# A mixed RWKV-7 and GatedDeltaNet layer on one core: the first branch's scan rebuilt on prepared transition matrices

## The chip, the core and the metric

The kernel runs on one core of one Trainium2 chip. The metric is the device time of one execution in microseconds. A matmul runs on TensorE (PE in the profile; its weight loads are PEld), elementwise work on VectorE (DVE), ScalarE (ACT) and GpSimd (POOL); SyncE (SP) issues most of the DMAs. Each engine works through its own instructions in order and waits on semaphores for what others have made.

## The reference

One layer over 256 latent tokens and 256 context tokens, width D = 2048. Latent and context tokens are normalised and modulated, projected by one weight `w_in`, and go through two token mixers, each in both directions. The context is scanned first and its final state starts the latent scan. Cut to what matters:

```python
mod = silu(c) @ w_ada + b_ada            # shifts, scales, gates (and the same for c_ctx)
h, hc = modulate(rmsnorm(x), ...), modulate(rmsnorm(ctx), ...)
rw, cv, z, ab, gt = split(h @ w_in)      # the same for hc

# first branch, RWKV-7: 16 heads of 64, per token and direction
def step(s, (r, w, k, v, kk, b)):        # s is 64 x 64
    sa = s @ kk
    s  = s * w - outer(sa, b) + outer(v, k)
    return s, s @ r

# second branch, gated DeltaNet (GDN): 8 heads of 128, in chunks of 64, with a
# triangular solve per chunk and a scan over chunks of the same kind
y = (sigmoid(g_a) * (o_a @ p_a) + sigmoid(g_b) * (o_b @ p_b)) @ w_out
x = x + gt1 * y
x = x + gt2 * swiglu(modulate(rmsnorm(x)))
return rmsnorm(x)
```

The decays `w` and the rates in `b` and `k` come from low-rank products (ranks 96, 96 and 64). All arithmetic is float32.

## The kernel before

A large projection is split: each float32 operand is a high and a low part of a faster type, and each k-tile of 128 takes three matmuls, `hxh` by `whi`, `hxl` by `whi`, `hxh` by `wlo`. One product has 16 k-tiles, so 48 matmuls, 512 columns wide (all tokens: the letters k, v, K, V) or 256 (latent tokens: r, Q and the gates g). `cast` loads its weights (`wraw`), rounds them to `whi` on ACT and subtracts on DVE to get `wlo`. Small matmuls are plain float32, and the profile shows two records for one of them.

The stages are, in order: modulation and the low-rank inputs (a first stage limited by the loads of `w_ada`, whose parts are woven with small products by the table `TILES`, lines 521 to 535); the weave, in which both branches run beside the projections; then the products with `p_a`, `p_b` and `w_out`, the FFN and the last norm.

In the weave, two RWKV heads make a pair, which occupies the 128 partitions, and there are 8 pairs. Tokens lie in 8 chunks of 64, the first four latent and the last four context. For pair `p` the work goes through generators:

- `prepare(p)` makes the keys, rates and decays: `exc` and `inc` are running products of decays up to and including a token, `et` their ends. It builds the operands: `LAl` (latent keys by `exc` and receptance by `inc`, in one tile per direction), `LAc` (context keys by `exc`), `ic` and `kt`.
- `grams(p, d)` multiplies them within a chunk, masks, and keeps the triangle `LT`, the masked products in place of `LAl`/`LAc`, and `Pm`; it turns `ic` and `kt` into `KB`.
- `inverse(p)` inverts the unit triangles (`invert`, by 16-token blocks, then 32, then 64) and multiplies the inverse into `KB` and `Pm`.
- `values(p)` (not changed) and `scan(p)`: the scan walks over 8 chunks in both directions at once, four context chunks and then four latent ones. `VX` holds state and values of a chunk. Per step, `VX` by `LAc` or `LAl` gives a first sum, which ACT copies into `VX`; a second group multiplies by `KB`, adds an identity product that carries the state, and DVE multiplies by `et` into the next `VX`. In the latent steps the readout (`LAl` by `VX`, then `Pm` by `VX`) is added and goes to `Y`.

GDN heads go through `tokens` (operands `keg`, `kta`), `head_grams`, `head_inverse` and `head_scan` (`NW` holds the products for the steps) in the same way, 8 heads in turn, after the last pairs.

What sets the order of instructions on PE, DVE and ACT is a planner, the class `Weave` (lines 185 to 281). Each generator yields one operation or a list for one engine; a tuple such as `("scan", p - 3)` waits until that name has been called ready, and a bank name waits for a free PSUM bank. The planner keeps a clock per engine with a cost for each operation, takes the operation that can start first, and breaks ties by rank (`RANK`, line 30: lower first). What it picks is written down as the program. Of the large products, `products` chooses the next one when the one before starts. The order of SP's queue follows from the same run, since the loads are issued as generators reach them.

## Time and profile before

| | |
|---|---|
| median of 3 runs | 2216.26 us (2205.15 to 2219.96) |
| the profiled execution | 2212.82 us, span 2211.0 us |
| PE busy | 2138.1 us (97%) |
| DVE busy | 1560.2 us (71%) |
| ACT busy | 1081.2 us (49%) |
| POOL busy | 93.6 us (4%) |
| DMA | mean 197 GB/s, 435.13 MB |

The first stage lasts to about 118 us, the weave from there to 1244 us, where the products with `p_a` begin; the FFN lies between 1452 and 1950 us, and the last product and norm behind it. The inverses of the 8 pairs end at 277, 353, 421, 488, 555, 623, 687 and 752 us and their scans at 312, 390, 461, 524, 595, 659, 723 and 789 us. The second branch's scans begin between 865 and 1261 us.

In a row of the profile `s<-VX,KB 128*64 128x64 f32 x8` means: written to `s` (a PSUM bank) from `VX` and `KB`, with 128 rows and 64 columns of the array in use, 128 partitions by 64 columns moving, eight records in a row. A start and a duration in us stand ahead; in square brackets stands the idle time before it and what ended it. L147 is the line of the planner's helper that issues every planned operation, so most rows of the weave have it. Durations of matmuls overlap, so lengths are taken from starts.

### The profile page before, as it was taken

The page shows a single profiled execution, that of the slowest core. Times are in us where ns is not written, and L with a number is a line of the kernel's source. Part 1 is how long each engine was busy: PE and PEld are TensorE (multiplying, and loading weights), DVE is VectorE, ACT ScalarE, POOL GpSimd, SP SyncE. Part 2 cuts the span into 40 slices and gives each one's busy share as a digit, 9 for nine tenths or more (in the row PEclk, how much of TensorE's full clock was granted, in tenths as well). Part 3 has the DMA queues.
Part 4 walks back from the last instruction along what each step waited for, and adds up shares of the span by engine and source line. Part 5 has one row for each costly group of instructions (what it writes and reads, how often), then busy time and mean ns, then how long its engine had stood idle before and what let it go on. Part 6 is the DMA issues. An engine that isn't in the chain of part 4 may idle for free. (4 is left out here: it accounts for less than half of the span.)

```text
span 2211.0 us, 54434 instructions
## 1 busy us (share of the span) xinstructions
PE 2138.1 (97%) x22780; PEld 1910.8 (86%) x22780; DVE 1560.2 (71%) x3245; ACT 1081.2 (49%) x1915; POOL 93.6 (4%) x171
## 2 busy tenths in 40 slices
PE   6998999999999999999899899999999999999998
PEld 4776678787788788887789799999999999999997
DVE  3456788888798577998998689956665655444444
ACT  3248745545456555454554465534444444444443
POOL 0000000000000010111110010100000000000000
PEclk9999899999999999999999999999999999999999
DMA  9966544444444355565567888927777776566665
GB/s 383 413 188 201 152 117 108 120 109 109 121 113 112 111 182 167 177 195 167 170 202 251 291 297 303 344 78 236 237 235 233 230 234 198 186 184 187 188 185 160
DMA packets 234486, 435.13 MB, mean 197 GB/s; under 512 B 115329, under 2 KB 129665, under 8 KB 229889
## 3 DMA queue, kind: packets, MB, share of 16 engines
q1 hardware_dynamic: 206304, 355.11, 51.1%
q0 software_dynamic: 14112, 51.39, 7.1%
q10 hardware_dynamic: 13824, 25.17, 3.4%
q8 instruction: 178, 2.92, 0.6%
q14 instruction: 68, 0.55, 0.1%
HBM read 405.76 MB, written 25.84 MB: 195 GB/s over the span
## 5 line engine op out<-in xcount | busy, mean ns | idle before, releaser
L371 DVE TENSOR_TENSOR wlo<-wraw,whi 128x1024 fp32r<-128x1024 f32 x328 | 392.7, 1198 | 319.5 <-ACT whi L370 317.4
L370 ACT CAST whi<-wraw 128x1024 fp32r<-128x1024 f32 x328 | 337.9, 1031 | 461.3 <-PE mm L381 410.6
L147 PE MATMUL mm<-hxh,wlo 128*128 128x256 f32 (+1 forms) x1376 | 460.6, 335 | 5.7 <-DVE wlo L147 5.5
L147 PE MATMUL mm<-hxh,whi 128*128 128x256 f32 (+1 forms) x1376 | 461.9, 336 | 0.9 <-ACT arena L147 0.5
L147 PE MATMUL mm<-hxl,whi 128*128 128x256 f32 (+1 forms) x1376 | 460.8, 335 | 0.0
L380 PE MATMUL mm<-hfh,whi 128*128 128x256 f32 x1344 | 376.8, 280 | 0.0
L381 PE MATMUL mm<-hfl,whi 128*128 128x256 f32 x1344 | 375.8, 280 | 0.0
L382 PE MATMUL mm<-hfh,wlo 128*128 128x256 f32 x1344 | 374.6, 279 | 0.1
L147 PEld LDWEIGHTS mm<-hxh,wlo 128*128 128x128 f32 x1376 | 260.1, 189 | 33.6 <-DVE wlo L147 8.4
L147 PEld LDWEIGHTS mm<-hxh,whi 128*128 128x128 f32 x1376 | 260.1, 189 | 27.1 <-issue 4.4
L147 PEld LDWEIGHTS mm<-hxl,whi 128*128 128x128 f32 x1376 | 260.2, 189 | 26.1 <-issue 6.2
L147 DVE TENSOR_TENSOR wlo<-wraw,whi 128x512 fp32r<-128x512 f32 x344 | 236.9, 691 | 49.5 <-ACT whi L147 48.0
L382 PEld LDWEIGHTS mm<-hfh,wlo 128*128 128x128 f32 x1344 | 252.6, 188 | 0.6 <-DVE wlo L371 0.5
L381 PEld LDWEIGHTS mm<-hfl,whi 128*128 128x128 f32 x1344 | 252.7, 188 | 0.0
L380 PEld LDWEIGHTS mm<-hfh,whi 128*128 128x128 f32 x1344 | 252.5, 188 | 0.0
L147 ACT CAST whi<-wraw 128x512 fp32r<-128x512 f32 x344 | 205.2, 616 | 96.2 <-PE mm L147 63.4
L147 DVE TENSOR_TENSOR arena<-arena 128x28 f32<-128x28 f32 (+13 forms) x538 | 132.1, 247 | 18.7 <-DMA arena<-scr 7.1
L380 PE MATMUL mm<-za,whi 128*128 128x256 f32 x512 | 144.0, 281 | 0.0
L381 PE MATMUL mm<-za,whi 128*128 128x256 f32 x512 | 143.3, 280 | 0.0
L382 PE MATMUL mm<-za,wlo 128*128 128x256 f32 x512 | 142.4, 278 | 0.0
L147 ACT ACTIVATE arena<-arena 128x512 f32<-128x512 f32 (+3 forms) x132 | 76.8, 592 | 40.1 <-DVE arena L147 37.3
L381 PEld LDWEIGHTS mm<-za,whi 128*128 128x128 f32 x512 | 96.3, 188 | 0.0
(329 smaller groups left out, 3911.3 us busy)
## 6 DMA issues: line engine op xcount, KB each, us to landing
wraw<-w SPq DMA_DIRECT2D x172, 512.0 KB, 4.3
wraw<-wgu SPq DMA_DIRECT2D x168, 512.0 KB, 4.7
aw<-ada_rest POOLq DMA_DIRECT2D x96, 512.0 KB, 5.5
aw<-ada_first SPq DMA_DIRECT2D x32, 1024.0 KB, 12.6
wraw<-wdn SPq DMA_DIRECT2D x64, 448.0 KB, 3.6
wraw<-wout SPq DMA_DIRECT2D x32, 512.0 KB, 6.3
aw<-ada_gt ACTq DMA_DIRECT2D x64, 256.0 KB, 4.9
wraw<-wdn SPq DMA_DIRECT2D x32, 512.0 KB, 3.6
```

Of the source, the lines that this page charges most:

```text
L147: return Op(self, cost, lambda: getattr(self.engine, name)(out, *a, **k), kind)
L370: S.copy(hi[:, c, :M], raw[:, c, :M])
L371: V.tensor_sub(lo[:, c, :M], raw[:, c, :M], hi[:, c, :M].bitcast(F32))
L380: E.matmul(ps, hi, Xh[:, k, :n], start=first and i == 0, stop=False)
L381: E.matmul(ps, hi, Xl[:, k, :n], start=False, stop=False)
L382: E.matmul(ps, lo, Xh[:, k, :n], start=False, stop=last and i == len(wt) - 1)
```

## The change

`prepare(p)` no longer makes `LAl` and `LAc`. It makes `kh` (all keys by `exc`, one 128x512 multiplication per direction) and `laR` (receptance by `inc`). For direction 0 it now waits for `scan(p-2)` instead of `scan(p-3)`, ahead of `et`, `kh` and `laR`.

`grams(p, d)` has a first group over all 8 chunks (`ic` by `kh`, `kh` by `kt`) and a second one with the receptance over the four latent chunks. The masked key product goes to a new tile `X`, into which `kh` is also turned (four more transposes and four ACT copies per direction). A new tile `KBx` is filled with identities by two POOL copies per pair; the turned `kt` goes into its other halves. It waits for `("mats", p - 2)` in direction 0 and for `("begun", p)` in direction 1.

`inverse(p)` ends with three more groups of 32 matmuls of 64x64x64, `X` by `KB` for each direction and `X` by `Pm`, each followed by two DVE additions of 512 columns into `KBx` and `laR`. After that, `KBx` holds for each chunk and direction a full 128x128 transition matrix. The copy of `Pm` moves from DVE to ACT, and `KB` is copied at once. In `invert` the second product of the 16-unit case is 64 matmuls of 32x32 by 16 columns instead of 32 of 64x64 by 16.

`scan(p)` has 7 steps, each of two matmuls 128x128x128 (one per direction) and two DVE multiplications by `et`, and then one readout of 16 matmuls into one bank and one `Y` copy.

In the second branch `NW` has three blocks instead of four per direction, `keg` and `kta` have 384 instead of 512 columns in half of their multiplications, and several buffers share the place of `X`. `products` chooses the next product at k-tile 4 of the current one instead of at its start, and r of a pair needs `("kgemm", p)` instead of `("prepared", p-1, 0)`. `TILES` and the loads of the first stage go in pairs.

```diff
--- invert, scan's waits, products, TILES
-        TILES = ((0, 0, 0, 0), (1, 1, 1, 1), ...
+        TILES = ((0, 0), (2, 2), (2, 2), (2, 2), (1, 3), (2, 2), (1, 3), (1, 2), (2, 2))
...
-        if nu == 16:
-            yield [e.matmul(pv[64 * h:64 * h + 64, 1, u], Tx[64 * h:64 * h + 64, u, :], Qm[64 * h:64 * h + 64, u, :],
-                            start=True, stop=True) for u in range(nu) for h in range(2)]
-        else:
-            yield [e.matmul(pv[r, 1, u], Tx[r, u, b:b + 32], Qm[r, u, :], start=True, stop=True) for h, u, b, r in fours]
+        yield [e.matmul(pv[r, 1, u], Tx[r, u, b:b + 32], Qm[r, u, :], start=True, stop=True) for h, u, b, r in fours]
...
                 if p > 1:
                     yield "inverse", p - 2
-                if p > 2:
-                    yield "scan", p - 3
+                if p > 1:
+                    yield "scan", p - 2
+                o["laR"] = la = rs.tile([P, 2, 4, 2, 64], F32, tag="laR", name="laR", bufs=2)
...
+            o["kh", d] = kh = rs.tile([P, 512], F32, tag="Kh", name="kh", bufs=2)
+            yield v.tensor_mul(c3(kh), c3(kk), exc)
             for j, h in enumerate(half):
-                yield v.tensor_mul(la[h, :, j, 0:64], c3(kk)[h, 0:4, :], exc[h, 0:4, :])
-                yield v.tensor_mul(la[h, :, j, 64:P], c3(r)[h], inc[h, 0:4, :])
-                yield v.tensor_mul(lc[h, :, j, :], c3(kk)[h, 4:8, :], exc[h, 4:8, :])
+                yield v.tensor_mul(la[h, d, :, j, :], c3(r)[h], inc[h, 0:4, :])
...
+        yield from turn(kh, 0, 4, lambda j, i, w: s.copy(X[half[1 - j], d, i::2, j, :], w))
         if d == 0:
             if p:
                 yield ("scan", p - 2) if p > 1 else ("lowrank", NPAIR - 1)
-            o["KB"] = rs.tile([P, 2, 8, 2, 64], F32, tag="KB", name="KB", bufs=2)
+            o["KB"] = rs.tile([P, 2, 8, 64], F32, tag="KB", name="KB", bufs=2)
+            o["KBx"] = KBx = rs.tile([P, 2, 8, 2, 64], F32, tag="KBx", name="KBx", bufs=2)
+            for j, h in enumerate(half):
+                G.tensor_copy(KBx[h, :, :, j, :].rearrange("p d c o -> p (d c) o"), ident[h, h].unsqueeze(1).to_broadcast([64, 16, 64]))
...
-        yield v.tensor_copy(Pm.rearrange("p d c k -> p (d c k)"), pm)
+        Pf = Pm.rearrange("p d c k -> p (d c k)")
+        yield [s.copy(Pf[half[1 - j]], pm[half[j]]) for j in range(2)]
         weave.release(pib)
         weave.ready("inverse", p)
+        for d in range(3):
+            ps = yield pab, pab
+            if d < 2:
+                yield quad([e.matmul(ps[j][r, 64 * c:64 * c + 64], X[half[1 - j], d, c, a], KB[half[1 - j], d, c, :],
+                                     start=True, stop=True) for c in range(8) for j in range(2) for a, r in enumerate(half)])
+                for j in range(2):
+                    yield v.tensor_add(KBx[:, d, :, j, :], c3(ps[j]), KBx[:, d, :, j, :])
+                    weave.release(pab)
+            else:
+                yield quad([e.matmul(ps[j][r, 64 * (4 * i + c):64 * (4 * i + c) + 64], X[half[1 - j], i, c, a], Pm[half[1 - j], i, c, :],
+                                     start=True, stop=True) for i in range(2) for c in range(4) for j in range(2) for a, r in enumerate(half)])
+                for j in range(2):
+                    t = la[:, :, :, j, :].rearrange("p d c k -> p (d c) k")
+                    yield v.tensor_add(t, c3(ps[j]), t)
+                    weave.release(pab)
+            if d == 1:
+                weave.ready("steps", p)
+        weave.ready("mats", p)
...
+        yield "steps", p
+        M, la, et = o["KBx"].rearrange("p d c j k -> p d c (j k)"), o["laR"], o["et"]
+        for n in range(7):
...
+            ps = yield psb
+            yield [e.matmul(ps[:, P * d:P * d + P], M[:, d, cs_[d]], vx[:, 4 * d + cm[d]].rearrange("p j k -> p (j k)"), start=True, stop=True)
+                   for d in range(2)]
...
             for j, h in enumerate(half):
-                yield s.copy(vx[h, both, j, :], c3(ps[h, 0:P]))
+                yield v.tensor_mul(vx[h, i:8 - i:7 - 2 * i, j, :], pv[h, :, j, :], end[h].to_broadcast([64, 2, 64]))
             weave.release(psb)
...
+        yield "mats", p
+        ps = yield psb
+        yield [e.matmul(ps[h, 64 * c:64 * c + 64], vx[:, 4 * d + c, j, :], la[:, d, c, j, :], start=c == 0 and d == 0, stop=c == 3 and d == 1)
+               for c in range(4) for d in range(2) for j, h in enumerate(half)]
...
-                todo.append(("r", p, ("prepared", p - 1, 0)))
+                todo.append(("r", p, ("kgemm", p)))
...
             for k in range(KT):
+                if k == 4:
+                    nxt = choose()
...
-        NW = gs.tile([P, 2, 4, P], F32, tag="NW", name="NW")
+        NW = gs.tile([P, 2, 3, P], F32, tag="NW", name="NW")
```

The change moves instructions, since the planner runs anew. On PE, in the middle of a scan, a piece of the order before (a name stands for its tile; `mm` is the bank of a large product, `s` that of a scan's step, and `x4` four matmuls in a row):

```order
L147 MATMUL s<-VX,LAc 64x64 x4
L147 MATMUL s<-VX,C 64x64 x4
L147 MATMUL mm<-hxh,whi 128x512
L147 MATMUL mm<-hxl,whi 128x512
L147 MATMUL mm<-hxh,wlo 128x512
L147 MATMUL mm<-hxh,whi 128x512
L147 MATMUL mm<-hxl,whi 128x512
L147 MATMUL s<-VX,KB 64x64 x4
L147 MATMUL mm<-hxh,wlo 128x512
```

and of the order now:

```order
L147 MATMUL s<-VX,KBx 128x128 x2
L147 MATMUL mm<-hxh,whi 128x512
L147 MATMUL mm<-hxl,whi 128x512
L147 MATMUL mm<-hxh,wlo 128x512
L147 MATMUL mm<-hxh,whi 128x512
L147 MATMUL mm<-hxl,whi 128x512
L147 MATMUL s<-VX,KBx 128x128 x2
```

A context step had two groups between products and now has one, with five product matmuls from one group to the next in both.

On DVE, at the end of a scan, a piece of the order before, in which `LAl` and `LAc` belong to a pair whose operands are being built and `VX` and `Y` to the scan:

```order
L147 COPY et<-arena 128x8
L147 TENSOR_TENSOR arena<-arena 128x48
L147 TENSOR_TENSOR LAl<-arena 64x4x64
L147 TENSOR_TENSOR arena<-arena 128x12x4
L147 TENSOR_TENSOR LAl<-arena 64x4x64
L147 TENSOR_TENSOR arena<-arena 128x55
L147 TENSOR_TENSOR LAc<-arena 64x4x64
```

and of the order now:

```order
L147 TENSOR_TENSOR VX<-s,et 64x2x64 x4
L147 COPY Y<-s 128x256
L147 STREAM_TRANSPOSE Tx<-arena 128x512
L147 COPY et<-arena 128x8
L147 STREAM_TRANSPOSE arena<-Tx 128x512
L147 TENSOR_TENSOR kh<-arena 128x512
L147 TENSOR_TENSOR laR<-arena 64x4x64 x2
L147 TENSOR_TENSOR wlo<-wraw,whi 128x512
```

Before, the operands were built among other steps of a scan; now `et`, `kh` and `laR` come behind the scan's `Y` copy, and a `wlo` for the large products stands behind them.

On SP, where the last low-rank weights (`lora`) are loaded at the start of the weave (`w` are the large products' weights, `sgd` and `scr` hold intermediate values in memory), before:

```order
L169 DMA wraw<-lora 96x1024
L169 DMA wraw<-w 128x1024 x2
L169 DMA arena<-sgd__1347 128x512 x2
L169 DMA scr_105<-arena 64x8x64 x3
L169 DMA wraw<-w 128x1024 x2
L169 DMA scr_105<-arena 64x8x64
L169 DMA arena<-sgd__1347 128x512
L169 DMA wraw<-lora 96x1024
```

and now:

```order
L169 DMA wraw<-lora 96x1024
L169 DMA arena<-sgd__1347 128x512
L169 DMA wraw<-lora 96x1024
L169 DMA arena<-sgd__1347 128x512
L169 DMA wraw<-w 128x1024
L169 DMA scr_105<-arena 64x8x64 x4
```

The last `lora` load stood behind three of the `scr` stores and now stands ahead of all four.

## The prediction

> **What bounds the kernel now.** I read the page's totals first, then the busy time by windows.

> ```profile
> span 2211.0 us, 54434 instructions
> PE 2138.1 (97%) x22780; PEld 1910.8 (86%) x22780; DVE 1560.2 (71%) x3245; ACT 1081.2 (49%) x1915; POOL 93.6 (4%) x171
> ...
> 300.00:400.00 100.00, 98.83 (x1443) 79.11 (x1442) 86.10 (x224) 52.87 (x123) 2.76 (x8) 1.00 0.43 116
> 1000.00:1100.00 100.00, 90.49 (x1002) 74.53 (x1001) 90.67 (x218) 49.26 (x96) 12.84 (x20) 1.00 0.58 175
> ```

> After the times of a window stand PE, PEld, DVE, ACT, POOL, the granted clock, the DMA share and GB/s. In the first branch (window from 300) PE is 98.8% busy at full clock: the large projections fill it wherever the small matmuls leave room. So work taken from PE there shortens the kernel by its own length, as long as nothing else becomes late. DVE is next with 86%. In the second branch (window from 1000), where DVE has 91%, PE falls to 90%.

> Next I read DVE's timeline for the marks of the pairs.

> ```profile
> 420.71 0.68 DVE L147 COPY Pm<-pi 128x512 f32<-128x512 f32 x1
> 441.71 0.41 DVE L147 TENSOR_TENSOR LAl<-arena 64x256 f32<-64x256 f32 x1
> 460.53 0.29 DVE L147 TENSOR_TENSOR Y<-s,Y 128x128 f32<-128x128 f32 x1
> 487.71 0.68 DVE L147 COPY Pm<-pi 128x512 f32<-128x512 f32 x1
> 554.88 0.68 DVE L147 COPY Pm<-pi 128x512 f32<-128x512 f32 x1
> 594.70 0.29 DVE L147 TENSOR_TENSOR Y<-s,Y 128x128 f32<-128x128 f32 x1
> ```

> Each `Pm<-pi` closes the inverse of a pair (here pairs 2, 3 and 4), and each last `Y` closes a scan (pairs 2 and 4). A pair takes (554.88−420.71)/2 = 67.1 us. A scan takes 594.70−554.88 = 39.8 us for 8 steps, 5.0 us each, of which PE works little (below). Pair 4's operands are begun at 441.71, 18.8 us before pair 2's scan ends.

> **The change part by part: PE.** A group of small matmuls costs PE the time that it puts between two products. I take it from starts: from the last product before to the second after, less two product intervals.

> ```profile
> 436.78 0.40 PE L147 MATMUL mm<-hxh,wlo 128*128 128x512 f32 x1
> 437.11 0.47 PE L147 MATMUL s<-VX,LAc 128*64 128x64 f32 x8
> ...
> 438.08 0.39 PE L147 MATMUL mm<-hxl,whi 128*128 128x512 f32 x1
> ...
> 438.77 0.40 PE L147 MATMUL mm<-hxl,whi 128*128 128x512 f32 x1
> ...
> 439.82 0.39 PE L147 MATMUL mm<-hxh,whi 128*128 128x512 f32 x1
> ...
> 440.29 0.40 PE L147 MATMUL mm<-hxh,wlo 128*128 128x512 f32 x1
> ...
> 441.80 0.39 PE L147 MATMUL mm<-hxl,whi 128*128 128x512 f32 x1
> ...
> 442.26 0.40 PE L147 MATMUL mm<-hxh,whi 128*128 128x512 f32 x1
> ...
> 443.68 0.39 PE L147 MATMUL mm<-hxh,wlo 128*128 128x512 f32 x1
> 443.91 0.39 PE L147 MATMUL mm<-hxh,whi 128*128 128x512 f32 x1
> ```

> A product follows the one before in 443.91−443.68 = 0.23 us. The four groups are: VX by LAc and by the identity, 438.08−436.78−0.46 = 0.84; VX by KB alone (8 records), 439.82−438.77−0.46 = 0.59; VX by LAl, identity and readout, 441.80−440.29−0.46 = 1.05; KB and Pm, 443.68−442.26−0.46 = 0.96. One matmul is two records. Eight records more, two abreast, cost 0.84−0.59 = 0.25: 0.0625 per beat of 64 columns, and the rest is the switch to and fro.

> *The old scan* per pair: step 0 has two groups of 0.59 (1.18), steps 1–3 have 0.84+0.59 (4.29), steps 4–6 have 1.05+0.96 (6.03), step 7 has 0.84+0.59 (1.43): 12.93, for 8 pairs **−103.4**.

> ```profile
> 395.06 0.39 PE L147 MATMUL mm<-hxh,wlo 128*128 128x512 f32 x1
> 395.38 1.26 PE L147 MATMUL pi<-arena 32*32 32x16 f32 x128
> ...
> 396.91 0.39 PE L147 MATMUL mm<-hxl,whi 128*128 128x512 f32 x1
> ...
> 397.98 0.48 PE L147 MATMUL mm<-hxh,wlo 128*128 128x512 f32 x1
> 398.39 2.04 PE L147 MATMUL pi<-arena,Tx 64*64 64x16 f32 x64
> ...
> 400.70 0.40 PE L147 MATMUL mm<-hxl,whi 128*128 128x512 f32 x1
> 400.93 0.40 PE L147 MATMUL mm<-hxh,wlo 128*128 128x512 f32 x1
> 401.26 0.69 PE L147 MATMUL pa<-LAc,arena 64*64 64x64 f32 x32
> ...
> 402.22 0.39 PE L147 MATMUL mm<-hxl,whi 128*128 128x512 f32 x1
> ...
> 986.99 0.39 PE L147 MATMUL mm<-hxl,whi 128*128 128x512 f32 x1
> 987.22 0.60 PE L147 MATMUL s<-Vn,kta 128*128 128x128 f32 x4
> ...
> 987.90 0.40 PE L147 MATMUL mm<-hxh,whi 128*128 128x512 f32 x1
> ```

> *The new step* is two full 128x128x128 matmuls, four records: the shape of Vn by kta in the second branch, 987.90−986.99−0.46 = 0.45. Seven steps and 8 pairs: **+25.2**. *The readout*: 32 records of 128x64, 16 beats instead of KB's 4, 0.59+12×0.0625 = 1.34; ×8 = **+10.7**. *The matrices* ("mats"): three groups a pair of 64 records of 64x64, ordered so that four share the array. 32 such records (LAc by arena) took 402.22−400.93−0.46 = 0.83; eight beats more make 1.33; ×24 = **+31.9**. *Turning kh*: four 128-column transposes per pair and direction, priced as the four records of 0.45; ×16 = **+7.2**. *The grams* stream as many columns as before, regrouped: 0 (upper bound, if the receptance group took eight beats more: 0.5×16 = 8). *The inverse's second product*: 64 of 64x64 by 16 columns took 400.70−397.98−0.46 = 2.26, and 128 of 32x32 take 396.91−395.06−0.46 = 1.39; ×8 = **−7.0**. *NW* has a block less per direction and head, two of four records' time, at most 0.22; ×16 = **−3.5**. The sum on PE is −38.9, of which −35.4 lies in the eight pairs: 4.4 per pair.

> **The other engines.** DVE: 160 operations of 64x256 or like width go and 72 come (at 0.41), 40 of 512 columns go and 112 come (at 0.68), 32 small Y additions go (0.29), and half of keg and kta shrink by a quarter (−2): −36.1+49.0−9.3−2 = +1.6 us. That is no load, but the pair is to become 4.4 us shorter with the same work: DVE goes from 86% to 86×67.1/62.7 = 92%, where the window from 1000 shows PE waiting. The window from 300 lost 1.2 us of PE in 100, the one from 1000 lost 9.5: between 0 and 15 us over the pairs' 8×62.7 = 500; I take **+8**, nearer the first row, since most of the second's wait comes in one stage with other chains. ACT loses the copies of `s` into VX and gains 64 copies of turned kh; with 53% it hides them (0). The next token product's weights are chosen at k-tile 4 rather than 0. Twelve k-tiles of three products remain, 12×3×0.23 = 8.3 us, for a cast and a difference: hidden, 0, and if the choice were late, about one operation of 0.68 per product.

> POOL gets two KBx copies of 64x1024 a pair.

> ```profile
> L852 POOL COPY bon<-arena 128x256 f32<-128x256 f32 x8 | 4.8, 598 | 357.1 <-DVE arena L147 357.1
> ...
> 223.78 2.08 PE L147 MATMUL s<-lin,wraw 96*128 96x512 f32 x2 [7.06 <-DMA wraw<-lora]
> ...
> 225.00:230.00 5.00, 3.63 (x14) 2.71 (x13) 2.03 (x9) 2.99 (x7) 0.00 (x0) 0.50 0.43 152
> 235.00:240.00 5.00, 5.00 (x15) 3.02 (x14) 2.57 (x12) 2.81 (x6) 0.00 (x0) 0.85 0.46 97
> ...
> 209.47 2.51 SPq L169 DMA_DIRECT2D scr<-arena  x3
> 215.27 1.01 SPq L169 DMA_DIRECT2D wraw<-lora  x1
> ```

> Four times the columns of `bon` make 2.4 us, 38 in all, on an engine busy 4%. Their first reader is the addition of the matrices, an inverse later; behind them in POOL's queue stand a small memset and the copy of `bon` for the next pair, which are no nearer. Priced 0; uncovered, 4.8 a pair.

> *The queue of SP.* PE stands 7.06 us before 223.78 because the last low-rank load is issued at 215.27, behind scr stores that wait from 209.47. Then the clock is 0.50. In the new order that load stands ahead of the stores. Stall and half clock together bound the gain: 7 us, and the 6 us or so that 12 us at half clock cost (223.78 to about 236: the window from 235 is back at 0.85 on the mean). So 0 to −13, **−6** taken: the products now left to fill the place are few, and what comes next is late too. [...]

> *The loads of the first stage* come in pairs, so PE changes between its two kinds of work less often there; no row of it is quoted, the loads set its pace, and I take −1 (0 to −3).

> *The second branch.* In PE's order 27 gate products of 256 columns (48 matmuls each) stood ahead of the last scan's end, and now 30. They are half as long as a 512-column matmul: 3×48×0.12 = 17 us of filler less for the second branch, where the window from 1000 already lacks 9.5. The first branch has that much less room for idle time, so most of it is only moved; I take **+5** (0 to 7: at worst a third more of the 9.5 in each of two such windows).

> *The wait that is added.* prepare(p) now waits for scan(p−2) instead of scan(p−3). In DVE's order the copy of et, kh, laR and then a wlo stand right behind the last Y copy; a late scan holds that wlo, and with it PE's products. Priced 0 in the forecast; below it is a rival.

> Sum against the profiled execution's 2212.8 us: −38.9+8+5−6−1 = −32.9, **2180 us**. The median of the runs, 2216.3, lies 3.5 above this execution; I forecast from the profiled one. Under 1% (22 us, so 2194.1 to 2238.4) counts as no change.

> **The rivals.**
> 1. *The loop over two pairs paces (16%).* Pair 4's operands to its inverse took 554.88−441.71 = 113.2 us, and the scan follows. With the added wait operands → inverse → scan → operands of p+2 is a ring. Against: the 113 us are mostly queueing; pair 3's inverse ends within them at 487.71. For: nothing in the trace of before tells how far they shrink. If the pairs then run no faster than now, six of them lose their 4.4: 2180+26 = 2206.
> 2. *The ring is longer than now (12%), slower.* It decides when new scan and matrices exceed 2×67.1−113.2 = 21 us with 113 unshrunk. The new scan has 7 hops of PE and DVE instead of 8 of PE, ACT, PE and DVE: half of 5.0 makes 17.5, and matrices and readout some 8 more. That is close. If hops take as long as before (36 us), a pair takes (113.2+36)/2 = 74.6, 7.5 more for six pairs: 2212.8+45−10 = 2248.
> 3. *DVE saturates (8%)*: the end of 15 us instead of 8, and 9 more for another 100 us like the window from 1000: 2196. [...]
> 4. *The matrices' matmuls don't go four abreast (4%).* Two abreast they take 16 beats more, 1.0 each: +24, 2204.

> **How the numbers follow.** The forecast's own case has 60%: 2180, from 2155 (8 and 5 falling away, −13 for the stall, −4 small) to 2194 (15 and 7 in full, no gain at the stall). Rivals 1, 3 and 4 (28%) lie at 2196 to 2206: same. Rival 2 (12%) is slower. The range 2152 to 2210 holds the first four, less their tails. Faster 0.60, same 0.28, slower 0.12.

> **What would show it.** Right: `s<-VX,KBx` groups of 4 records that delay products by 0.45; `KBx`-building groups of 64 records at 1.33; PE still 98% busy from 300 to 700, a pair at 62 to 63 us; no stall of 7 us by 224. Rival 1 or 2: PE waiting for `wlo` behind et and kh, right after a Y copy, and 67 us or more per pair. [...] Rival 4: the 64-record groups at 2.3. Wrong altogether if the time is below 2150, which no term here could give.

## The result: 0.7% slower, 2228 us for 2216

The changed kernel took 2228.24 us (median of 9 runs) beside 2215.76 us of the kernel before on the same chip: a ratio of 1.0068, with a 95% interval of 1.0044 to 1.0093. The forecast was 2180 us, with a range from 2152 to 2210. The time lies outside the range, on the other side of the kernel before, though by less than the 1% that was set as a change.

The page of the changed kernel, its totals and the row of queue q8, of the kind "instruction" (the kernel before has 178 packets and 2.92 MB there):

```profile
span 2226.1 us, 56729 instructions
PE 2117.7 (95%) x23996; PEld 1913.4 (86%) x23996; DVE 1571.3 (71%) x3197; ACT 1068.5 (48%) x1853; POOL 120.4 (5%) x203
...
q8 instruction: 188, 3.08, 0.6%
```

PE is busy for 20 us less, and the span is 15 us longer. The windows that the prediction read, and the one from 400 beside them, first that one in the kernel before:

```profile
400.00:500.00 100.00, 99.49 (x1578) 81.14 (x1574) 85.35 (x204) 52.11 (x124) 4.05 (x10) 1.00 0.42 116
```

and the three in the changed kernel:

```profile
300.00:400.00 100.00, 94.10 (x1441) 78.67 (x1439) 84.48 (x196) 45.83 (x102) 10.94 (x16) 0.98 0.39 108
400.00:500.00 100.00, 90.15 (x1755) 77.70 (x1757) 78.44 (x175) 46.98 (x106) 6.27 (x14) 0.93 0.43 114
1000.00:1100.00 100.00, 94.19 (x1021) 78.41 (x1020) 92.67 (x250) 51.69 (x101) 13.01 (x20) 1.00 0.59 175
```

In these two windows of the first branch PE was 98.8 and 99.5% busy at full clock. Now it is 90 to 94% busy, at a mean clock of 0.93 to 0.98 (in the three windows behind them, 94.6 to 98.7%). DVE did not fill up: it is busy for 78 to 84%, less than before. The window of the second branch is no worse than it was.

The whole loss arises between 118 us and the first product with `p_a`: 1126.2 us before, 1147.2 after. From there to the end the changed kernel is 5.9 us shorter. To see what that stretch consists of, I added up the intervals from start to start on PE by what they belong to, with intervals at half clock counted as half, and the other half as a term of its own:

| us between 118 us and the first product with `p_a` | before | after | difference |
|---|---|---|---|
| large products at their plain rate | 662.6 | 663.0 | +0.4 |
| scan and readout | 104.7 | 42.0 | −62.7 |
| the matrices (`X` by `KB` and by `Pm`) | 0 | 30.7 | +30.7 |
| turning `kh` | 0 | 7.2 | +7.2 |
| 16-column products of the inverses | 41.5 | 36.3 | −5.2 |
| grams | 34.1 | 36.1 | +2.0 |
| NW | 12.9 | 11.1 | −1.8 |
| all other small matmuls | 224.9 | 230.3 | +5.4 |
| lost to half clock | 9.2 | 25.5 | +16.3 |
| PE idle | 35.3 | 64.2 | +28.9 |

The groups that the change touches did become shorter, by 29.8 us. (The 5.4 us of other work is mostly a piece of the last GDN head that now comes ahead of the mark. The `NW` of this head is in the changed kernel's 11.1 us too, so that row compares eight heads with seven: per head it went from 1.84 to 1.39 us.) Idle time and half clock took 45 us. The waits of PE, longest first, show what is new. The one row of "issue" in the kernel before, and the changed kernel's waits:

```profile
PE pi L147 <- issue: 0.2, 1, 0.2
```

```profile
PE pi L147 <- issue: 11.8, 8, 2.2
...
PE mm L147 <- DVE wlo L147: 9.2, 13, 2.0
...
PE pi L147 <- DVE arena L147: 5.4, 11, 1.0
PE pa L147 <- DVE arena L147: 4.7, 5, 1.5
...
PE pa L147 <- issue: 4.1, 3, 1.8
PE pa L147 <- ACT KBx L147: 3.2, 1, 3.2
...
PE s L147 <- DMA wraw<-lora: 2.4, 1, 2.4
```

The columns are the total, the number of times and the longest. "Issue" means that PE waited for no other engine that the trace knows; in this stretch the kernel before has 0.2 us of it, the changed one 15.8. One such stop, in PE's timeline:

```profile
315.73 1.14 PE L147 MATMUL pi<-arena 32*32 32x16 f32 x114
317.36 0.31 PE L147 MATMUL pi<-arena 32*32 32x16 f32 x14 [0.48 <-issue]
317.60 1.15 PE L147 MATMUL s<-laR,VX 128*64 128x64 f32 x32
318.68 0.88 PE L147 MATMUL pi<-arena,Tx 32*32 32x16 f32 x82
321.63 0.57 PE L147 MATMUL pi<-arena,Tx 32*32 32x16 f32 x46 [2.08 <-issue]
322.13 0.70 PE L147 MATMUL pa<-sgd,g 64*128 64x256 f32 x2
322.76 0.66 PE L147 MATMUL pa<-C,arena 128*128 128x128 f32 x2
323.07 0.77 PE L147 MATMUL mm<-hxh,whi 128*128 128x512 f32 x1
323.64 0.63 PE L147 MATMUL mm<-hxl,whi 128*128 128x512 f32 x1
324.07 0.63 PE L147 MATMUL mm<-hxh,wlo 128*128 128x512 f32 x1
```

The inverse's second 16-column product, now 128 records, breaks off after 82 of them, in the middle of one list of matmuls whose operands are all there. It goes on 2.08 us later. Then the products come 0.43 us apart (324.07−323.64) where the plain interval is 0.23: the trace's clock is 0.50 from 322.8 to 326.2 us. In the trace's packets of queue q8, whole blocks of 16,384 bytes begin at 315.0, 319.3 and 323.3 us; the stop ends 2.3 us after the second of them begins. From the page, 3.08 MB over 2×23,996 matmuls and weight loads make 64 bytes each, by which a block holds an estimated 256. That gave a first theory, "supply": the two products alone are 512 instructions within 4 us, and blocks never come closer than 3.3 us in the twenty traces of this case. The rival, "ring", was rivals 1 and 2 of the prediction: the wait for `scan(p-2)` paces the pairs.

### The profile page after: what moved, and what is told of

Same layout as the page of the kernel before. It is cut to its first block, busy times and chain, and to the rows that moved or that the text cites. A ratio compares the mean times of both kernels' runs of the same rounds, so it can differ in the third digit from the quotient of the medians.

```text
span 2226.1 us, 56729 instructions
## 1 busy us (share of the span) xinstructions
PE 2117.7 (95%) x23996; PEld 1913.4 (86%) x23996; DVE 1571.3 (71%) x3197; ACT 1068.5 (48%) x1853; POOL 120.4 (5%) x203
## 3 DMA queue, kind: packets, MB, share of 16 engines
q8 instruction: 188, 3.08, 0.6%
## 4 chain that ended last, share of the span: by engine, by line
issue 45%; PE 29%; DVE 12%; DMA 9%; ACT 3%; POOL 1%; SPq 1%; POOLq 0%; DVEq 0%; ACTq 0%
PE mm L147 14%; PE pa L147 5%; DVE arena L147 4%; DVE wlo L147 2%; PE s L147 2%; PE pi L147 2%; PE mm L382 1%; PE mm L381 1%; PE mm L380 1%; DMA aw<-ada_rest 1%; DMA aw<-ada_first 1%; DVE aw L147 1%; ACT arena L147 1%; PE mm L475 1%; DMA wr<-wgu 1%
## 5 line engine op out<-in xcount | busy, mean ns | idle before, releaser
L147 PE MATMUL mm<-hxh,wlo 128*128 128x256 f32 (+1 forms) x1376 | 465.3, 338 | 10.0 <-DVE wlo L147 9.2
L147 PE MATMUL mm<-hxh,whi 128*128 128x256 f32 (+1 forms) x1376 | 463.8, 337 | 2.0 <-DVE arena L147 1.2
L147 PE MATMUL mm<-hxl,whi 128*128 128x256 f32 (+1 forms) x1376 | 461.1, 335 | 0.0
L147 PEld LDWEIGHTS mm<-hxh,wlo 128*128 128x128 f32 x1376 | 263.1, 191 | 39.6 <-DVE wlo L147 14.4
L147 PEld LDWEIGHTS mm<-hxh,whi 128*128 128x128 f32 x1376 | 263.3, 191 | 25.6 <-issue 5.6
L147 PEld LDWEIGHTS mm<-hxl,whi 128*128 128x128 f32 x1376 | 263.4, 191 | 23.6 <-issue 3.9
L147 DVE TENSOR_TENSOR wlo<-wraw,whi 128x512 fp32r<-128x512 f32 x344 | 239.9, 698 | 34.9 <-ACT whi L147 33.5
L147 ACT CAST whi<-wraw 128x512 fp32r<-128x512 f32 x344 | 204.5, 616 | 110.6 <-PE mm L147 84.4
L147 DVE TENSOR_TENSOR arena<-arena 128x28 f32<-128x28 f32 (+12 forms) x538 | 139.0, 261 | 23.5 <-DMA arena<-scr 9.2
L147 ACT ACTIVATE arena<-arena 128x512 f32<-128x512 f32 (+2 forms) x132 | 76.4, 593 | 76.4 <-DVE arena L147 59.5
```

The source lines that it names most:

```text
L147: return Op(self, cost, lambda: getattr(self.engine, name)(out, *a, **k), kind)
```

## The experiments

### One part undone or alone, planned anew

The inverse's second product back in its old form in the changed kernel (e1); both 16-column products in two halves with a pause between (e2); the new form alone in the kernel before (e3); and a control (e4) with the same instructions in another order.

```diff
 e1   restores the branch "if nu == 16" with 32 matmuls 64x64 in invert
 e2  -        yield [e.matmul(pv[r, 1, u], Tx[r, u, b:b + 32], Qm[r, u, :], ...) for h, u, b, r in fours]
     +        yield from spread([e.matmul(...) for h, u, b, r in fours], 32, 1.0)    # 32 at a time, pause 1 us
 e3   before.py with the single line "for h, u, b, r in fours" in place of that branch
 e4  -turn=0.17)
     +turn=0.171)
```

> The changed kernel with one part undone: the second product of the 16-unit inverse is again 32 matmuls of 64x64 by 16 columns, as in the kernel before. Theory 'supply': PE runs out of instructions after dense bursts of small matmuls (its fetch brings 16 KB, 256 instructions, each 3.4 to 4 us, and a burst of 64 matmuls of 32x32 is 256 instructions in 1.4 us), so with the sparser form the idle time put down to issue falls from 15.8 us to 5 or less, half of the short stretches at half clock go, and the time falls by 10 to 20 us in spite of 7 us more PE work: 2208 to 2218. Rival 'ring' (the wait of prepare(p) for scan(p-2) paces the pairs, and the stops before the inverse are its consequence): nothing but the 7 us of PE work comes back, 2228 to 2236, and the issue gaps stay above 10 us.

> The changed kernel with both 16-unit products of the inverse given out in two halves of 32 matmuls with a planned pause of 1 us between, which large products fill. The same work is done. 'Supply': issue idle falls to 5 us or less, time 2203 to 2216. 'Ring': each inverse gets 2 us longer, so 2228 to 2240.

> The kernel before with one part of the change alone: the second product of the 16-unit inverse as 64 matmuls of 32x32. 'Supply': issue idle appears (5 us or more where the kernel before has 0.2), and the 7 us of PE work saved are given back: 2212 to 2226. 'Ring', or any theory in which the bursts are harmless: 7 us less, 2206 to 2211.

> The changed kernel with the planner's cost of a turn between kinds of matmuls at 0.171 instead of 0.17 us: the same instructions, planned in another order from the middle of the third pair on. It tells how much an order by itself is worth. 'Supply' and 'ring' both expect 2228 within 6 us and issue idle of 10 to 20 us; if it lands 10 us or more away, single runs of re-planned kernels can't carry differences of that size.

| | us | ratio to before | PE idle | of it issue | lost to half clock |
|---|---|---|---|---|---|
| kernel before | 2216 | 1 | 35.3 | 0.2 | 9.2 |
| changed | 2228 | 1.0068 | 64.2 | 15.8 | 25.5 |
| e1, old form | 2243 | 1.0126 (1.0102–1.0151) | 61.2 | 5.7 | 32.6 |
| e2, two halves | 2228 | 1.0054 (1.0036–1.0071) | 51.7 | 5.9 | 30.4 |
| e3, before with the new form | 2250 | 1.016 (1.0135–1.0185) | 55.6 | 7.3 | 20.7 |
| e4, control | 2223 | 1.0028 (1.0008–1.0048) | 61.2 | 19.6 | 26.6 |

The issue time moved the way that "supply" had it in e1, e2 and e3, though e1 and e2 stay just above the 5 us that were named. The times fit neither theory: e1 was to be 2208 to 2218 or 2228 to 2236, e3 was 24 us above the higher of its two ranges, and e2's 2228 stands at the lower edge of "ring". Each of these kernels had been planned anew, and in all of them PE idles and slows down more than in the kernel before. Hence a third theory, "order": the kernel before has a lucky order, and every other order loses.

### The same instructions in another order

A thousandth of a microsecond in one of the planner's constants changes no instruction, only their order. The constants are the cost of a turn between kinds of matmuls (turn), the delay between engines (hop) and the delay behind an operation of the same engine (own). The kernel before was moved in three ways, and the changed one in the same three (the turn is e4).

```diff
 b_turn, e4_control  -turn=0.17)    +turn=0.171)
 b_hop, a_hop        -hop=0.255     +hop=0.256
 b_own, a_own        -own=0.092     +own=0.093
```

> The kernel before with the planner's cost of a turn at 0.171 instead of 0.17 us, nothing else: the same instructions in another order from the first pair on. Theory 'order' (new here: the order that the kernel before has sits well with the chip, and any re-planned one has some 20 us more of idle PE and 10 to 20 us more at half clock, as all four runs so far had): 2228 to 2250, idle of PE from 118 us to the products with p_a of 50 us or more, where the kernel before has 35. Theory 'bursts' (the dense groups of small matmuls that the change brings stop PE): the kernel before has none of them, 2210 to 2222, idle near 35, issue idle below 1.

> The kernel before with the planner's delay between engines at 0.256 instead of 0.255 us, nothing else. A second draw of the same question. 'Order': 2228 to 2250. 'Bursts': 2210 to 2222.

> The kernel before with the planner's delay behind an operation of the same engine at 0.093 instead of 0.092 us, nothing else. A third draw. 'Order': 2228 to 2250. 'Bursts': 2210 to 2222.

> The changed kernel with the planner's delay between engines at 0.256 instead of 0.255 us: a third order of it beside the changed kernel itself and the one with the turn at 0.171. Both theories: 2215 to 2240. With 'order' the changed kernels as a set lie below the re-planned kernels before as a set, by about the 30 us of PE work that the groups of the change save; with 'bursts' they lie 5 us or more above them.

> The changed kernel with the planner's delay behind an operation of the same engine at 0.093 instead of 0.092 us: with the turn at 0.171 and the delay between engines at 0.256 it makes three re-planned changed kernels against three re-planned kernels before (2254, 2230, 2243 us, mean 2242). 'Order': 2215 to 2245, so that the three changed ones have a mean of 2220 to 2237, 5 to 22 us below the three before. 'Bursts' (the groups of the change cost more than they save): 2240 or more, and no gain of the means.

| | kernel before, us | ratio | idle, half clock | changed kernel, us | ratio | idle, half clock |
|---|---|---|---|---|---|---|
| own constants | 2216 | 1 | 35.3, 9.2 | 2228 | 1.0068 | 64.2, 25.5 |
| turn | 2254 | 1.017 (1.0139–1.0201) | 60.6, 34.6 | 2223 | 1.0028 (1.0008–1.0048) | 61.2, 26.6 |
| hop | 2230 | 1.0064 (1.0035–1.0093) | 46.6, 22.9 | 2241 | 1.0116 (1.0083–1.0149) | 65.9, 30.8 |
| own | 2243 | 1.0113 (1.0068–1.0159) | 43.5, 25.3 | 2249 | 1.0145 (1.0104–1.0187) | 64.9, 28.7 |

All three moved kernels before are slower, by 14 to 37 us, with nothing changed but the order. The three moved kernels before have a mean of 2242 us, the three moved changed ones 2238. That was to be 5 to 22 us apart by "order"; it is 4, and single draws lie 23 to 26 us apart, so these six runs don't tell the two programs apart. (a_own's 2249 lies above the range of "order" and within that of "bursts", the theory that the dense groups of the change cost more than they save.) What they do show is that the time in which PE is not idle is 1106 us on the mean of the three moved kernels before and 1084 in the changed ones (22 us less), and idle time is 50 against 64 (14 us more). The first row compares the best order of one program among four with an ordinary order of the other.

In the moved kernels before the long stops are mostly other ones than in the changed kernel. The longest waits inside the weave of the one with the moved turn:

```profile
PE mm L147 <- DVE wlo L147: 12.7, 10, 4.0
...
PE pi L147 <- DVE arena L147: 6.7, 8, 1.6
PE s L147 <- DMA wraw<-lora: 6.6, 2, 5.6
```

Issue is 6.1 us there. So there are two things, order and dense groups, and runs that plan anew mix them. A planner's rule against dense groups did not separate them either:

```diff
+    held = self.hold and lane is self.tensor and w[5][0].kind != "split"
+    key = (start + 1.5 * held, w[0], start)            # small matmuls wait while a product can go
+    self.hold = self.debt > 0.8 or self.hold and self.debt > 0.2   # debt: small us less product us; d_05: 0.5, 0.1
```

> The changed kernel with one more rule in the planner: once PE has had more than 0.8 us of small matmuls (by the planner's costs, large products taken off against them), further groups of small ones are put back by up to 1.5 us while a large product can go, until the balance is 0.2 us. The largest group of small matmuls between two products falls from 162 to 93 matmuls, and the groups grow from 396 to 419, so some 8 us more of switching. If dense groups make the issue idle and with it half clock: issue idle from 15.8 to 6 or less, half-clock time from 54 to 35 us or less, 2205 to 2222. 'Order' alone: a draw like any other, 2220 to 2245, and half-clock time as before.

> The same rule at 0.5 and 0.1 us: the largest group is 66 matmuls, 453 groups, so some 20 us more of switching on PE. If dense groups are the cause of issue idle and half clock: issue idle 3 or less, half-clock time 30 us or less, 2210 to 2230. 'Order' alone: 2235 to 2260, since nothing pays for the switching.

> The kernel before with the same rule at 0.8 and 0.2 us (436 groups of small matmuls for 421). 'Order': a draw of the kernel before, 2228 to 2255. If dense groups are what costs in re-planned orders of either kernel: 2215 to 2230, half-clock time 30 us or less.

The three took 2249 (1.0139), 2248 (1.0149) and 2269 us (1.0232): the first two are as slow as the slowest order of the changed kernel without the rule (2249), the third is slower than that of the kernel before (2254). Issue time fell only with the stricter rule (13.9 us in d_08, 4.9 in d_05), and there `wlo` became the longest wait (16.6 us). Every expectation of a gain missed.

### The order kept to the instruction

The planner can be left to plan one form while the program is written with another. Then every other instruction keeps its place.

```diff
 x1 (kernel before): plan 32 matmuls 64x64, write each as two of 32x32
+    op.call = lambda u=u, h=h: [e.engine.matmul(pv[r, 1, u], Tx[r, u, b:b + 32], Qm[r, u, :], ...) for b in (0, 32) ...][-1]
 x2 (changed kernel), x3 (changed kernel, turn 0.171): plan 64 of 32x32, write each pair as one of 64x64
+    op.call = (lambda: None) if b else lambda u=u, r=r: e.engine.matmul(pv[r, 1, u], Tx[r, u, :], Qm[r, u, :], ...)
```

> The kernel before, planned exactly as it is, so that every other instruction keeps its place; only in writing the program each 64x64 matmul of the inverse's second product becomes two of 32x32. It is the earlier run with this form alone without the new order. 'Order' (the earlier run's 34 us came from re-planning): 2208 to 2222, far below that run's 2250. 'Bursts' as the cause of the 34 us: 2240 or more. Issue idle tells whether 512 instructions in two bursts outrun PE's supply in this order: 0 to 2 us if the order leaves room between, 5 or more if not.

> The changed kernel, planned exactly as it is; only in writing the program each pair of 32x32 matmuls of the inverse's second product becomes one of 64x64 (half the instructions, 5 us more PE work). If PE's instruction supply makes the issue stops: issue idle from 15.8 to 6 us or less, half-clock time from 54 to 40 us or less, 2210 to 2223. If the stops are waits for something else that the profile doesn't show: issue idle stays above 10, 2228 to 2238.

> The same edit on the changed kernel planned with the turn at 0.171 us (2223 us, issue idle 19.6). Supply: issue idle 7 us or less, 2205 to 2218, which would be level with the kernel before or under it. Otherwise 2223 to 2233.

| | us, ratio | issue | idle | half clock |
|---|---|---|---|---|
| before → x1 | 2218 → 2241, 1.0107 (1.0080–1.0134) | 0.2 → 16.1 | 35.3 → 50.7 | 9.2 → 20.2 |
| changed → x2 | 2228 → 2220, 1.0011 (0.9988–1.0035) | 15.8 → 6.2 | 64.2 → 51.1 | 25.5 → 20.4 |
| e4 → x3 | 2223 → 2216, 0.9995 (0.9971–1.0018) | 19.6 → 4.7 | 61.2 → 50.4 | 26.6 → 20.7 |

Here the dense product stands by itself. In an unchanged order, 8 products written as 128 instead of 64 records cost the kernel before some 24 us, though by the prediction's rows the form in 128 records is the shorter one (1.39 us for 2.26). I had expected 2208 to 2222 from "order", and "order" is wrong for this run. PE's waits in x1, and one of them:

```profile
PE pi L147 <- issue: 5.5, 4, 3.3
PE pi L645 <- issue: 5.4, 4, 2.1
...
327.38 1.32 PE L147 MATMUL pi<-arena 32*32 32x16 f32 x116
331.96 0.40 PE L147 MATMUL pi<-arena 32*32 32x16 f32 x12 [3.26 <-issue]
332.29 1.22 PE L147 MATMUL pa<-bon,C 128*128 128x256 f32 x2
332.95 0.99 PE L147 MATMUL mm<-hxh,whi 128*128 128x512 f32 x1
333.74 0.63 PE L147 MATMUL mm<-hxl,whi 128*128 128x512 f32 x1
334.16 0.63 PE L147 MATMUL mm<-hxh,wlo 128*128 128x512 f32 x1
```

L645 is the rewritten product, and L147 the one before it, whose 128 records the kernel before also had without a stop: it now breaks off as well. The time lost to half clock rises too, from 9.2 to 20.2 us. Taking the 128 records back out of the changed kernel gains some 8 us by the medians in two orders (2228 to 2220, 2223 to 2216); by the ratios to the kernel before it is 13 and 7 us, and in the second order the two intervals overlap. Both are then level with the kernel before. The same edit planned anew (e1) had lost 14 us. So e1 and x2, which have the same instructions in two orders, lie 23 us apart.

The traces also show where the issue stops stand. Between 118 us and the first product with `p_a`, the twenty traces have 141 of them, and 139 end 2.2 to 3.4 us after a block of q8 begins; of the 1259 stops put down to another engine or a DMA, 99 do. In the changed kernel four pairs of neighbouring stops stand exactly 128 records of PE apart (records 3269 and 3397, 4793 and 4921, 5809 and 5937, 8222 and 8350): with their weight loads 256 instructions, one block. That stops stand a block's length apart and end soon after a block begins is what "supply" would have; what PE does inside such a stop, no trace shows. The moved kernels before have such stops too: 5 of the 6 in the one with the moved turn.

### Fewer instructions for the matrices

In the same kept orders, the matrices' matmuls that differ only in the column half were written as one of 64 rows by 128 columns (y1 on x3, y2 on x2).

```diff
+    ops[2 * i].call = lambda o=o, l=l, r=r: e.engine.matmul(o, l, r, ...)   # l: X[half, d, c], 64 x 128
+    ops[2 * i + 1].call = lambda: None
```

> The changed kernel planned with the turn at 0.171 us and the inverse's second product in 64x64 form (2216 us, issue idle 4.7), order kept to the instruction; in writing the program, each pair of matmuls of the matrices that differ only in the column half becomes one of 64 rows by 128 columns: 32 instructions in place of 64 per group, 768 fewer in all, the same columns streamed. Supply: issue idle from 4.7 to 3 us or less, half-clock time no longer, 2208 to 2217. If fewer instructions don't matter any more, or 64 by 128 shares the array worse: 2216 to 2226.

> The same on the changed kernel's own order with the 64x64 form (2220 us, issue idle 6.2). Supply: issue idle 4 us or less, 2211 to 2220. Otherwise 2220 to 2230.

They took 2233 us (1.0069) and 2242 us (1.0112), above both ranges of each. One group in x3, and the same group in y1:

```profile
445.74 0.40 PE L147 MATMUL mm<-hxl,whi 128*128 128x512 f32 x1
446.07 1.16 PE L147 MATMUL pa<-KB,X 64*64 64x64 f32 x64
447.16 0.50 PE L147 MATMUL mm<-hxh,wlo 128*128 128x512 f32 x1
447.50 0.39 PE L147 MATMUL mm<-hxh,whi 128*128 128x512 f32 x1
```

```profile
444.84 0.39 PE L147 MATMUL mm<-hxl,whi 128*128 128x512 f32 x1
445.16 2.00 PE L926 MATMUL pa<-KB,X 64*128 64x64 f32 x32
447.09 0.51 PE L147 MATMUL mm<-hxh,wlo 128*128 128x512 f32 x1
447.43 0.39 PE L147 MATMUL mm<-hxh,whi 128*128 128x512 f32 x1
```

By the prediction's arithmetic the 64 records cost 447.50−445.74−0.46 = 1.30 us and the 32 wider ones 447.43−444.84−0.46 = 2.13. Half the records take 0.83 us longer: with 64 rows by 128 columns the group gains nothing from having fewer of them. That is 24×0.83 = 20 us more work, and the issue time rose (from 4.7 and 6.2 us to 10.5 and 10.6). As a test of "supply" the runs are spoilt by that price.

### The added wait taken back

This run starts from x3 and is planned anew.

```diff
-                if p > 1:
-                    yield "scan", p - 2
+                if p > 2:
+                    yield "scan", p - 3
-  ... tag="laR", name="laR", bufs=2)
+  ... tag="laR", name="laR", bufs=3)     # paid with one buffer less of Pm and kh
```

> The changed kernel with the turn at 0.171 us and the 64x64 form (2216 us), and the added wait taken back as far as space allows: a third buffer for laR, so that prepare(p) waits for scan(p-3) again ahead of et, kh and laR (paid for with one buffer less of Pm and of kh; kh of direction 1 waits until that of direction 0 is turned; the turning of ic and kt still waits for scan(p-2)). The kernel is planned anew. 'Ring' (the wait for scan(p-2) closes a ring of operands, inverse and scan, and paces the pairs): a pair takes 70 us or less on the mean from the third scan's end to the seventh's, where it takes 72.8, the last scan ends before 800 us where it ends at 808, and the time is 2195 to 2210. 'Order' (the ring costs nothing that a re-planned order doesn't cost anyway): 2215 to 2245, with idle of PE at 45 to 65 us.

In the changed kernel the ring is closed without slack, as DVE's timeline shows at the end of two scans, two pairs apart:

```profile
467.50 0.42 DVE L147 COPY Y<-s 128x256 f32<-128x256 f32 x1
467.84 0.16 DVE L147 COPY et<-arena 128x8 f32<-128x8 f32 x1
467.91 0.68 DVE L147 TENSOR_TENSOR kh<-arena 128x512 f32<-128x512 f32 x1
...
611.09 0.42 DVE L147 COPY Y<-s 128x256 f32<-128x256 f32 x1 [0.78 <-PE s L147]
611.43 0.16 DVE L147 COPY et<-arena 128x8 f32<-128x8 f32 x1
611.51 0.68 DVE L147 TENSOR_TENSOR kh<-arena 128x512 f32<-128x512 f32 x1
```

`kh` is built right behind `Y`, and the ring from 467.91 to 611.51 takes 143.6 us, 71.8 for a pair. Without the wait a pair takes 70.2 us instead of the 72.8 of x3, and the last scan ends at 788 us instead of 808, much as "ring" had it. But the kernel takes 2214 us (0.9992, 0.9973 to 1.0011), where "ring" had 2195 to 2210: the ring paces the pairs, and loosening it gained nothing in this order. (Since orders of one program differ by 20 us and more, a price of the ring that the new order hides is not excluded.) While the pairs wait, PE is given gate products, 30 of them ahead of the last scan's end in x3 and 27 here; they are then missing later, for from the first `NW` product to the first with `p_a` x3 takes 369 us and this run 388. None of the versions beats the kernel before clearly; x2, x3 and this one are level with it.

## Why the prediction was wrong

*What bounds the kernel.* Right as far as it went: PE is the bound, and its groups became shorter. "Work taken from PE there shortens the kernel by its own length, as long as nothing else becomes late" is the step that failed. It took the stretch with 98.8% busy as a property of the stage. It is a property of one order: the same program in three other orders idles 8 to 25 us more and loses 14 to 25 us more to half clock.

*The prices on PE.* The undisturbed medians of the changed kernel: the step 0.45 us (forecast 0.45; of the 40 steps that stand alone between two products, 15 took this, and the others 0.55 to 1.14), the readout 1.28 (1.34), a matrix group 1.29 (1.33), turning `kh` 0.45 (0.45), NW 0.22 less per direction (0.22). The sum was −38.9 and came to −29.8. Scan and readout together measured 42.0 us for 35.9, and the grams +2.0 for 0; the inverse gave 1.8 us less than forecast. `NW` seems to give 1.7 us less only because of the mark: per head it is what was forecast.

*"128 of 32x32 take 1.39, −7.0".* The price of the array was right, with −5.2 us measured. What was left out is that they are 256 instructions in 1.4 us, behind another 256. In an unchanged order this edit costs the kernel before 24 us, and taking it back gains 8 us in the changed one. This is the clearest single error.

*Idle time +8 (0 to 15).* It was laid on DVE, and it measured +28.9: issue +15.6, waits for DVE's results in `arena` +7.3, for `wlo` +3.7, one stop of 3.2 us for `KBx`, and smaller ones, less 5.7 us at the low-rank load. DVE is not saturated (78 to 86%), so rival 3 is out. The two `wlo` subtractions that overlap a `KBx` copy did take 1.52 us each, though, where the median is 0.68. All DVE operations beside these copies together are 11.8 us longer than their medians. The short waits for `arena` and `wlo` look like those of an order that fits less well, as in the moved kernels before; that was not tested, and some may come from these longer operations.

*The queue of SP (−6).* Right for the stop: 8.1 us of waiting for `lora` fell to 2.4, and the stretch of 17.1 us at half clock is gone. Three others, of 3.4, 3.4 and 10.2 us, stand between 206 and 255 us in its place.

*Half clock.* The forecast had it once, as something to win. It is +16.3 us net: 11 stretches for 3. Up to the first product with `p_a` the stretches at 0.50 of both kernels last 3.41 us or a multiple of it, and the 17.1 us of the kernel before (219.4 to 236.5 us) are five of them, each behind a window of 3.4 us in which PE idled for 17% or more (78, 100, 29, 29 and 17%).

*The second branch (+5, with NW −3.5).* From the first `NW` product to the first product with `p_a` it took 379.1 us before and 380.8 after: right in number. Little rests on it, since versions of the changed kernel take 369 (e4, x3) to 388 (the run without the wait).

*The rivals.* The mechanism of rivals 1 and 2 is there (the ring takes 143.6 us for two pairs, 67.1 a pair became 71.8; on the mean from the third scan's end to the seventh's, 65.6 became 73.6, near the 74.6 of rival 2). Its price did not show in the one order tried: the run without the wait is 2 us faster than the one with it, inside the noise. Rival 4 did not happen (1.29 us). POOL's KBx copies took 1.2 us each, half the estimate. No rival had what happened: an order that fits less well, and groups of 256 instructions in 1.4 us where the blocks of q8 come 3.3 us apart or more.

*What stays open.* Why the order of the kernel before fits so well is not settled; that it is an outlier among the orders of its own program is shown by three draws. The 12 us between the two kernels are made of both causes: some 8 us by the medians, 13 by the ratios, go with the dense product, and the rest is within what re-planning does. Whether the changed program has an order as good as that of the kernel before, and would then show its 30 us, was not tried.

## What to carry to other kernels

Where a scheduler sets the order, test a change against re-planned versions of the old kernel too: here a constant moved by 0.001 us is worth 14 to 37 us, more than the change. Better still, keep the planned order and change only how an operation is written. And price small matmuls by their number as well as by their columns: here 8 products of 256 instructions in 1.4 us each, in an unchanged order, brought the kernel before 15.9 us more issue time (0.2 to 16.1) and 11.0 us more lost to half clock (9.2 to 20.2).

## What the runs showed of the hardware

*Blocks of q8 and issue stops.* In the twenty traces the packets of q8, whose kind on the page is "instruction", have 16,384 bytes, with 254 to 256 matmuls and weight loads for one of them (45,432 to 47,992 in all), and no two begin closer than 3.3 us to each other. Of the 141 issue stops, 139 ended 2.2 to 3.4 us after a block began. The kernel before has 178 blocks, 3.4 to 4.1 us apart at four places between 320 and 490 us, and no stop there.

```profile
731.40:734.80 3.40, 3.19 (x70) 2.66 (x68) 1.86 (x10) 0.00 (x0) 1.05 (x1) 1.00 0.68 215
734.80:738.20 3.40, 3.40 (x15) 3.11 (x14) 0.61 (x4) 1.28 (x6) 0.00 (x0) 0.50 0.03 9
738.20:741.60 3.40, 3.40 (x10) 2.63 (x9) 1.71 (x2) 1.67 (x7) 0.00 (x0) 0.50 0.00 0
741.60:745.00 3.40, 3.40 (x137) 2.46 (x136) 2.96 (x6) 0.49 (x1) 0.00 (x0) 1.00 0.26 45
```

In the changed kernel the stop of 2.08 us that ends at 321.63 lies in the window from 319.4, in which PE is busy for 1.34 us of 3.41; the next one, from 322.8 to 326.2, is at 0.50. From the 0.50 over 3.41 us I estimate the price of that window at 1.7 us, on top of the stop.

*DVE beside a POOL copy.* In the changed kernel the two `wlo<-wraw,whi` subtractions beside a `KBx` copy took 1.52 us each, where the median of this shape is 0.68, while a `Tx<-arena` transpose and four copies `arena<-pi` beside `KBx` kept their times (0.71 and 0.28 us).

*The form of the matrices' matmuls.* By the prediction's arithmetic, 32 records of 64 rows by 128 columns cost 2.13 us (y1), and 64 records of 64x64 with the same columns 1.30 us (x3).
